# Seven block products for eight in five of 22 up-projection pairs, and shorter down chunks

## The chip, the cores and the metric

The kernel runs on one core of one Trainium2 chip. The metric is the device time of one execution in microseconds (us), the median of three runs. Five engines work side by side, each through its own queue in order: TensorE (PE, with PEld for its weight loads), VectorE (DVE), ScalarE (ACT), GpSimd (POOL) and SyncE (SP, which here only issues DMAs).

## The reference

Two layers of a decoder trunk on 512 tokens, width 1024, all in float32. Each layer is a mixer (state-space scan and stick-breaking attention in layer 0, a matrix-memory mixer in layer 1) and then a gated convolution FFN. The change touches only the FFN:

```python
def conv_ffn(h, up_w, conv_w, conv_b, down_w):
    u = causal_dwconv(h @ up_w, conv_w, conv_b)      # up_w: 1024 x 5632
    gate, val = jnp.split(u, 2, axis=-1)
    return (jax.nn.silu(gate) * val) @ down_w        # down_w: 2816 x 1024
...
        h = h + conv_ffn(rmsnorm(h, norm_w[layer, 1]), ffn_up_w[layer], ...)
```

## The kernel before

Activations lie as features on the 128 partitions and 512 tokens along the row. A float32 product is made of three fp32r matmuls (`mm3`): high part by high part, high by low, low by high. Every weight tile is therefore split first: ACT copies it into `hi`, DVE subtracts to get `lo`; `W_BUFS` = 5 such tiles can be ready ahead of PE, and two `raw` tiles receive them from DRAM.

**Up projection.** The 2816 gate and 2816 value columns are 22 tiles of 128 each; tile j of both makes one *pair*. A plain tile (`feat`) is 8 k-tiles times 3 matmuls of 512 columns, so a pair is 48 matmuls. DVE multiplies the result by the row factor `rb` (the norm), ACT and DVE make the width-3 convolution, ACT the SiLU, DVE the product of gate and value.

**Down projection.** For the first 16 of the 22 k-tiles, in two chunks of 8 (`CHUNKS`), the product is done in 2 x 2 blocks (two k-tiles, two output tiles, two halves of the tokens) with 7 block products for 8 (a Strassen form): `token_sums` makes the seven sums of the activations (`11`, `21`, `22`, `n1`, `n2`, `t3`, `t4`; tiles `B`, `s`, `F`, `G`), `weight_tiles` the sums of the weights (`P1` to `P4`; two of them begin as an accumulating DMA that POOL issues, two are DVE adds), and `down_blocks` runs, for each of four *slices* c (two output tiles), seven products of (k-tiles / 2) x 3 matmuls of 256 columns into PSUM tiles X, Y and Z. DVE adds each result to the residual `h` as it comes; as X and Y go on accumulating, such a read must be done before the next product into the same tile. The last 6 k-tiles (`REST`) are plain (`down_rest`).

The residual `h` (8 tiles) stays in SBUF throughout. All activations, sums and `P` tiles share 71 slots, which come free in the order in which they were asked for.

**What sets the order.** The program is recorded first, and `Recorder.order` then places every call: each engine takes, of the calls whose inputs are ready by the table of costs in the code, the one that was written first. The queues then run in that order; an SP row that waits holds every DMA behind it.

Of the kernel before, what the change touches and what calls it, by code (L numbers as in the profile page):

```python
# [15 lines left out]
F32 = mybir.dt.float32  # L16
F32R = mybir.dt.float32r
AF = mybir.ActivationFunctionType
ALU = mybir.AluOpType
# [3 lines left out]
P = 128  # L23
T = 512
NB = 4
KD = 8
EPS = 1e-6
FF = 22
# [4 lines left out]
def _feat(w):  # L33

    k, n = w.shape
    return list(w.reshape(k // P, P, n // P, P).transpose(2, 1, 0, 3))
# [48 lines left out]
def _ffn_units(i, l):  # L85
    u = []
    up = _feat(i["ffn_up_w"][l])
    dn = i["ffn_down_w"][l]
    for kind, n in FFN_PLAN:
        if kind == "up":  # L90
            u += [up[n], up[FF + n]]
        elif kind == "down":
            a, b = CHUNKS[n]

            t = dn[a * P : b * P].reshape((b - a) // 2, 2, P, 4, 2, P).transpose(3, 2, 4, 1, 0, 5)
            u += [x.reshape(P, 4, (b - a) // 2, P) for x in t]
        else:
            u += _feat(dn[REST * P :])
    return u

CHUNKS = [(0, 8), (8, 16)]
REST = 16
FFN_PLAN = [("up", j) for j in range(9)] + [("down", 0)] + [("up", j) for j in range(9, 17)] + [("down", 1)]
FFN_PLAN += [("up", j) for j in range(17, FF)] + [("rest", 0)]

X = lambda kind, *ns: [(kind, n) for n in ns]
# [161 lines left out]
class Recorder:  # L273
# [5 lines left out]
    def add(self, engine, method, args, kw):  # L279
        c = Call()  # L280
        c.engine, c.method, c.args, c.kw, c.i = engine, method, args, kw, len(self.calls)
        views = [a for a in args if isinstance(a, View)] + [a for a in kw.values() if isinstance(a, View)]
        c.outs, c.ins = views[:1], views[1:]
        c.func = next((a for a in args if a in TABLES), None) if method == "activation" else None
        c.cost = self.cost(c)
        self.calls.append(c)
# [162 lines left out]
class Net:  # L449
# [65 lines left out]
    def weight_tiles(self):  # L515

        v = self.nc.vector
        while self.wi < len(self.sizes):
            n, blocks = self.sizes[self.wi]
            if not blocks:  # L520
                yield self.split_weights([self.load_unit(self.raw_tile())])
                continue
            src, kb = self.next_unit(), n // 4
            r1, r2 = self.raw_tile(), self.raw_tile()[:, 0:kb]
            self.nc.sync.dma_start(r1, src[:, 0 : 2 * kb])
            p1, p2, p3, p4 = (self.slot(f"P{k}") for k in (1, 2, 3, 4))
            yield self.split_weights([r1])

            for p, i in ((p1, 3), (p3, 0)):
                self.nc.sync.dma_start(p, src[:, 2 * kb : 3 * kb])  # L530
                self.nc.gpsimd.dma_start(p, src[:, i * kb : (i + 1) * kb], accum_op=ALU.add)
            v.tensor_tensor(p2, p1, r1[:, 0:kb], op=ALU.add)
            yield self.split_weights([p2, p1])
            v.tensor_tensor(p4, p2, r1[:, kb : 2 * kb], op=ALU.add)
            self.nc.sync.dma_start(r2, src[:, 3 * kb : n])
            yield self.split_weights([p3, p4])
            yield self.split_weights([r2])
# [634 lines left out]


    def ffn(self, l, h, last):
        nc = self.nc
        xs, _, _, rb = self.norm(h, f"nw{l}1")
        pairs, ss, first = {}, [], None
        for kind, j in FFN_PLAN:
            if kind == "down":
                a, b = CHUNKS[j]  # L1180
                for c in range(4):
                    self.down_blocks([pairs[k] for k in range(a // 2, b // 2)], h, c)
                continue
            if kind == "rest":
                self.down_rest(ss, h, last)
                continue
            cc = []
            for part in range(2):
                n = j + part * FF
                ps = self.ps(("pj", "zz", "yy")[self.n % 3])  # L1190
                self.feat(ps, xs)
                u, c = self.slot("u"), self.slot("c")
                nc.vector.tensor_tensor(u, ps, rb, op=ALU.mult)
                nc.scalar.activation(c, u, AF.Identity, scale=self.param(f"fw{l}2", n), bias=self.param(f"fb{l}", n))
                for d in (1, 2):
                    nc.vector.scalar_tensor_tensor(c[:, d:T], u[:, 0 : T - d], self.param(f"fw{l}{2 - d}", n), c[:, d:T],
                                                   op0=ALU.mult, op1=ALU.add)
                cc.append(c)
            nc.scalar.activation(cc[0], cc[0], AF.Silu)
            nc.vector.tensor_tensor(cc[1], cc[0], cc[1], op=ALU.mult)  # L1200
            if j >= REST:
                ss.append(self.split(cc[1], "s"))
            elif j % 2:
                pairs[j // 2] = self.token_sums(first, cc[1])
            else:
                first = cc[1]

    def token_sums(self, c1, c2):

        v = self.nc.vector  # L1210
        a, b = slice(0, T // 2), slice(T // 2, T)
        t = self.slot("B11", F32R)
        self.nc.scalar.copy(t[:, a], c1[:, a])
        v.tensor_tensor(t[:, b], c1[:, a], t[:, a].bitcast(F32), op=ALU.subtract)
        s2 = self.split(c2, "s")
        f, g = self.slot("F"), self.slot("G")
        v.tensor_tensor(f[:, a], c1[:, a], c1[:, b], op=ALU.subtract)
        v.scalar_tensor_tensor(f[:, b], c2[:, b], -1.0, f[:, a], op0=ALU.mult, op1=ALU.subtract)
        fs = self.split(f, "F")
        v.tensor_tensor(g[:, a], c2[:, b], c1[:, b], op=ALU.subtract)  # L1220
        v.scalar_tensor_tensor(g[:, b], f[:, b], -1.0, c2[:, a], op0=ALU.mult, op1=ALU.subtract)
        gs = self.split(g, "G")
        half = lambda t, s: (t[0][:, s], t[1][:, s])
        return {"11": (t[:, a], t[:, b]), "21": half(s2, a), "22": half(s2, b),
                "n1": half(fs, a), "n2": half(fs, b), "t3": half(gs, a), "t4": half(gs, b)}

    def down_blocks(self, xs, h, c):

        v = self.nc.vector
        kb, n = len(xs) * P, T // 2
        a, b = slice(0, n), slice(n, T)
        X, Z, Y = (self.ps(t)[:, 0:n] for t in (("pj", "yy", "zz"), ("yy", "pj", "pj"))[c % 2])
        h1, h2 = h[2 * c], h[2 * c + 1]
        at = {"i": 0, "u": None}

        def product(ps, form, more=False):
            i = at["i"]  # L1240
            if i % 2 == 0:
                at["u"] = self.unit()
            hi, lo = at["u"]
            at["i"] = i + 1
            for k, x in enumerate(xs):
                s = slice(i % 2 * kb + k * P, i % 2 * kb + k * P + P)
                self.mm3(ps, (hi[:, s], lo[:, s]), x[form], not more and k == 0, k == len(xs) - 1, skip_group_check=more)

        add = lambda o, ps, op=ALU.add: v.tensor_tensor(o, o, ps, op=op)
        product(X, "11")  # L1250
        product(Z, "21")
        add(h1[:, a], X)
        product(X, "n2", True)
        add(h1[:, a], Z)
        product(Y, "n1")
        add(h1[:, b], X)
        product(X, "t3", True)
        add(h2[:, b], Y, ALU.subtract)
        product(Y, "22", True)
        add(h2[:, b], X, ALU.subtract)  # L1260
        product(X, "t4", True)
        add(h1[:, b], Y)
        add(h2[:, a], X, ALU.subtract)

    def down_rest(self, ss, h, last):
        nc = self.nc
        for c in range(8):
            ps = self.ps(("pj", "zz", "yy", "tt")[c % 4])
            self.feat(ps, ss)
            nc.vector.tensor_tensor(h[c], ps, h[c], op=ALU.add)  # L1270
            if last:
                nc.sync.dma_start(self.out[c], h[c])

    def load_x(self, a=0, b=KD):
        h = []
# [6 lines left out]
    def run(self):  # L1282
        nc = self.nc
# [4 lines left out]
        ps = self.ps()  # L1288
# [4 lines left out]
        h, raw = [], []  # L1293
# [4 lines left out]
        xs, w0 = [], []  # L1298
# [9 lines left out]
        xs, var, r, rb = self.norm(h, "nw00", xs)  # L1308
# [57 lines left out]
        h = S["h"]  # L1366
        yb = S.get("yb", [])
        yb += [self.split(self.ysb[k], "yb") for k in range(len(yb), 8)]
        for c in range(8):
            if ("b", c) in S:  # L1370
                pb, u = S["b", c]
# [3 lines left out]
                self.feat(pb, yb)  # L1375
            nc.vector.tensor_tensor(h[c], pb, h[c], op=ALU.add)
        S.clear()
        self.ffn(0, h, False)


        xs, var, r, rb = self.norm(h, "nw10")
# [23 lines left out]
        a, b, c = L1_CUTS  # L1405
# [13 lines left out]
        for c in range(8):  # L1419
            if c < OUT_SPLIT:  # L1420
                ps, u = begun[c]
                self.feat(ps, ys, u, tiles=range(4, 8))
            else:
                ps = self.ps(("pj", "zz", "yy", "tt")[c % 4])
# [59 lines left out]
```

## Time and profile before

| what | value |
|---|---|
| median of 3 runs | 1389.71 us (1389.37 to 1391.11) |
| profiled execution, own time | 1389.56 us |
| its span, first to last instruction | 1387.8 us |
| PE / DVE / ACT busy | 1376.7 / 1116.2 / 783.9 us |
| DMA | 147.96 MB, mean 107 GB/s |

A busy PE is a modelled figure, so the waits of PE are read from the chain and from the spacing of its groups. The FFN of layer 0 begins at about 463 us of the span and ends at about 811; that of layer 1 runs from about 1032 to the end.

### The profile page before, as it was taken

What the parts mean: (1) busy time and instruction counts of PE and PEld (TensorE: products, weight loads), DVE (VectorE), ACT (ScalarE), POOL (GpSimd) and SP (SyncE); (2) the same over time, 40 slices, a digit from 0 to 9 for tenths busy, and PEclk for the clock granted to TensorE, in tenths of its full rate; (3) what the DMA queues carried; (4) which work ended last, traced back from release to release, by engine and by line L of the source; (5) the groups of instructions that cost most, each with busy time, mean ns of one, the idle gap of its engine ahead of it and who ended that gap; (6) DMA issues with size and microseconds to landing.
All of it is one profiled execution on the core that took longest, in us unless ns stands there. A gap on an engine that the chain in (4) does not pass through costs nothing.

```text
span 1387.8 us, 20206 instructions
## 1 busy us (share of the span) xinstructions
PE 1376.7 (99%) x7491; PEld 1185.3 (85%) x7491; DVE 1116.2 (80%) x1963; ACT 783.9 (56%) x1325; POOL 87.1 (6%) x172
## 2 busy tenths in 40 slices
PE   9999999999999999999999999999999999999998
PEld 8898998989788888988898898888888899889887
DVE  7999889999997778878877657798758886888662
ACT  7798997786665444344434446776434444444440
POOL 0000001201120001000100000110000010010000
PEclk9999999999999999999999999999999999999999
DMA  6423223223312345243532225222234354443422
GB/s 220 130 77 112 86 78 98 70 83 132 98 46 91 101 127 137 92 138 113 129 122 95 81 82 171 77 92 89 65 106 126 102 129 129 122 133 95 137 68 84
DMA packets 53617, 147.96 MB, mean 107 GB/s; under 512 B 6136, under 2 KB 7160, under 8 KB 53520
## 3 DMA queue, kind: packets, MB, share of 16 engines
q1 hardware_dynamic: 48912, 138.29, 31.4%
q0 software_dynamic: 4608, 8.39, 3.7%
q8 instruction: 59, 0.97, 0.3%
q14 instruction: 38, 0.31, 0.1%
HBM read 141.36 MB, written 2.15 MB: 103 GB/s over the span
## 4 chain that ended last, share of the span: by engine, by line
PE 88%; DVE 5%; issue 3%; ACT 3%; POOL 1%; DMA 0%; SPq 0%; DVEq 0%; POOLq 0%; ACTq 0%
PE pj L436 43%; PE yy L436 26%; PE zz L436 14%; PE tt L436 5%; DVE gt L436 1%; DVE wt L436 1%; DVE lo L436 1%; DVE wTl L436 0%; ACT L436 0%; ACT Kh L436 0%; DMA h<-in_xT 0%; POOL wt L436 0%; ACT Q L436 0%; DVE ss L436 0%; ACT hi L436 0%
## 5 line engine op out<-in xcount | busy, mean ns | idle before, releaser
L436 ACT CAST hi<-raw 128x1024 fp32r<-128x1024 f32 (+2 forms) x236 | 227.8, 968 | 257.2 <-PE yy L436 58.6
L436 DVE TENSOR_TENSOR lo<-raw,hi 128x1024 fp32r<-128x1024 f32 (+2 forms) x236 | 263.8, 1120 | 25.2 <-ACT hi L436 24.5
L436 PE MATMUL pj<-xnh,hi 128*128 128x512 f32 x488 | 194.1, 398 | 0.0
L436 PE MATMUL pj<-xnh,lo 128*128 128x512 f32 x488 | 193.9, 397 | 0.0
L436 PE MATMUL pj<-xnl,hi 128*128 128x512 f32 x488 | 193.5, 396 | 0.0
L436 DVE SCALAR_TENSOR_TENSOR c<-u,pp,c 128x511 f32<-128x511 f32 (+2 forms) x212 | 158.0, 748 | 3.9 <-ACT c L436 1.6
L436 PE MATMUL yy<-xnl,hi 128*128 128x512 f32 x320 | 126.4, 395 | 0.0
L436 PE MATMUL yy<-xnh,lo 128*128 128x512 f32 x320 | 126.2, 394 | 0.0
L436 PE MATMUL yy<-xnh,hi 128*128 128x512 f32 x320 | 125.6, 392 | 0.0
L436 PE MATMUL pj<-lo,xnh 128*128 128x384 f32 (+2 forms) x320 | 108.6, 340 | 0.0
L436 PEld LDWEIGHTS pj<-xnh,lo 128*128 128x128 f32 x488 | 91.8, 188 | 19.1
L436 PEld LDWEIGHTS pj<-xnl,hi 128*128 128x128 f32 x488 | 91.8, 188 | 18.9
L436 PEld LDWEIGHTS pj<-xnh,hi 128*128 128x128 f32 x488 | 91.9, 188 | 18.8 <-issue 0.2
L436 PE MATMUL pj<-hi,xnl 128*128 128x384 f32 (+2 forms) x320 | 107.2, 336 | 0.0
L436 PE MATMUL pj<-hi,xnh 128*128 128x384 f32 (+2 forms) x320 | 106.8, 338 | 0.0
L436 ACT ACTIVATE c<-u,pp 128x512 f32<-128x512 f32 x100 | 81.1, 813 | 9.7 <-DVE u L436 8.3
L436 PE MATMUL zz<-xnl,hi 128*128 128x512 f32 x184 | 72.7, 395 | 0.0
L436 PE MATMUL zz<-xnh,lo 128*128 128x512 f32 x184 | 72.5, 394 | 0.0
L436 PE MATMUL zz<-xnh,hi 128*128 128x512 f32 x184 | 72.2, 392 | 0.0
L436 PEld LDWEIGHTS yy<-xnh,hi 128*128 128x128 f32 x320 | 60.2, 188 | 14.0
L436 PEld LDWEIGHTS yy<-xnl,hi 128*128 128x128 f32 x320 | 60.1, 188 | 13.9
L436 PEld LDWEIGHTS yy<-xnh,lo 128*128 128x128 f32 x320 | 60.1, 188 | 13.3
(418 smaller groups left out, 3330.7 us busy)
## 6 DMA issues: line engine op xcount, KB each, us to landing
raw<-in_w SPq DMA_DIRECT2D x168, 512.0 KB, 3.4
raw<-in_w SPq DMA_DIRECT2D x44, 384.0 KB, 3.1
P<-in_w SPq DMA_DIRECT2D x32, 256.0 KB, 5.6
P<-in_w POOLq DMA_DIRECT2D x32, 256.0 KB, 6.8
h<-in_xT SPq DMA_DIRECT2D x16, 256.0 KB, 4.7
E<-acsd SPq DMA_DIRECT2D x16, 256.0 KB, 3.9
raw<-in_w SPq DMA_DIRECT2D x16, 256.0 KB, 3.1
raw<-in_w SPq DMA_DIRECT2D x8, 264.0 KB, 2.7
```

The source lines that it names most:

```text
L436: getattr(getattr(nc, c.engine), c.method)(*(r(a) for a in c.args), **{k: r(v) for k, v in c.kw.items()})
```

## The change

In pairs 7, 10, 13, 16 and 19 (`UP_BLOCKS`) of each layer, gate and value tile together are the two outputs of a block product over k in four groups of two k-tiles: 7 products of 4 x 3 matmuls of 256 columns, 84 in all, stand for the 48 of 512 columns. For that, four `("x", n)` steps between the first up tiles scale `h` by the norm's weight and run `token_sums` on it (the parts `11`, `21`, `22` are views of the split `xn` that is there already; `F` and `G` are new). The weights of such a pair come through the block path of `weight_tiles`. Results are read out by ACT (four copies) and DVE (three adds), and then multiplied by `rb`.

The down projection becomes three chunks of 6 k-tiles and 4 plain ones. The residual goes to DRAM tiles `hd` when the FFN begins; each slice loads its two tiles, adds, and stores them back, and `down_rest` loads all eight.

```diff
+        if kind == "up" and n in UP_BLOCKS:
+            u.append(np.stack([up[m][:, k::2] for m in (n, FF + n) for k in range(2)], axis=1))
...
-CHUNKS = [(0, 8), (8, 16)]
-REST = 16
+CHUNKS = [(0, 6), (6, 12), (12, 18)]
+REST = 18
+UP_BLOCKS = (7, 10, 13, 16, 19)
...
+        hd = [self.dram.tile([P, T], F32, name=self.name("hd")) for _ in range(KD)]
+        for k in range(KD):
+            nc.sync.dma_start(hd[k], h[k])
...
+            if kind == "x":
+                hw = []
+                for k in (2 * j, 2 * j + 1):
+                    hw.append(self.slot("hw"))
+                    v.tensor_scalar(hw[-1], h[k], self.param(f"nw{l}1", k), None, op0=ALU.mult)
+                xb.append(self.token_sums(*hw, xs[2 * j], xs[2 * j + 1]))
...
                 for c in range(4):
-                    self.down_blocks([pairs[k] for k in range(a // 2, b // 2)], h, c)
+                    if c < 3:
+                        load(c + 1)
+                    self.down_blocks([pairs[k] for k in range(a // 2, b // 2)], *loaded[c], c)
+                    for e in range(2):
+                        nc.sync.dma_start(hd[2 * c + e], loaded[c][e])
...
+    def up_blocks(self, xs, rb, c):
+            if name in ("X1", "X2"):
+                nc.scalar.copy(u1[:, a if name == "X1" else b], ps)
+            elif name in ("Y1", "X4"):
+                nc.scalar.activation(u2[:, b if name == "Y1" else a], ps, AF.Copy, scale=-1.0)
+            elif name == "X3":
+                v.tensor_tensor(u2[:, b], u2[:, b], ps, op=ALU.subtract)
+            else:
+                o = u1[:, a if name == "Z" else b]
+                v.tensor_tensor(o, o, ps, op=ALU.add)
```

How the queues change, at three places. First PE, in the up projection. Before, a tile is 24 matmuls of 512 columns, of which these are the first five (`xnh`, `xnl` are the halves of the split activations; all have such names before the change):

```order
L436 MATMUL yy_6913<-xnh_5207,hi_6764 128x512
L436 MATMUL yy_6913<-xnl_5240,hi_6764 128x512
L436 MATMUL yy_6913<-xnh_5207,lo_6773 128x512
L436 MATMUL yy_6913<-xnh_5212,hi_6764 128x512
L436 MATMUL yy_6913<-xnl_5247,hi_6764 128x512
```

In pair 10 of the change, where the first block product (into `pj`) ends and the second (into `yy`) begins:

```order
L442 MATMUL pj_6881<-xnh_5382,hi_6740 128x256
L442 MATMUL pj_6881<-xnl_5398,hi_6740 128x256
L442 MATMUL pj_6881<-xnh_5382,lo_6751 128x256
L442 MATMUL yy_6901<-xnh_5216,hi_6740 128x256
L442 MATMUL yy_6901<-xnl_5251,hi_6740 128x256
L442 MATMUL yy_6901<-xnh_5216,lo_6751 128x256
```

The matmuls are half as wide, and 12 of them make a product where 24 made a tile. In the whole program PE gets 7911 matmuls for 7479.

Second DVE, in a down chunk of layer 0. Before (chunk 0, third slice; `h` rows read a product, `lo` rows split weights):

```order
L436 TENSOR_TENSOR lo_6500<-raw_6400,hi_6481 128x1024
L436 TENSOR_TENSOR h_4095<-h_4095,yy_6486 128x256
L436 TENSOR_TENSOR lo_6521<-P_1348_6449,hi_6505 128x512
L436 TENSOR_TENSOR h_4095<-h_4095,pj_6419 128x256
L436 TENSOR_TENSOR lo_6521<-P_1347_6154,hi_6505 128x512
L436 TENSOR_TENSOR lo_6550<-P_1349_6162,hi_6539 128x512
L436 TENSOR_TENSOR h_4107<-h_4107,zz_6524 128x256
L436 TENSOR_TENSOR h_4107<-h_4107,pj_6419 128x256
```

And after the change (chunk 1, third slice):

```order
L442 TENSOR_TENSOR P_1556_7492<-P_1555_7350,raw_7438 128x384
L442 TENSOR_TENSOR h_7196<-h_7196,yy_7409 128x256
L442 TENSOR_TENSOR P_1558_7507<-P_1556_7492,raw_7438 128x384
L442 TENSOR_TENSOR lo_7513<-raw_7438,hi_7490 128x768
L442 TENSOR_TENSOR lo_7526<-P_1556_7492,hi_7505 128x384
L442 TENSOR_TENSOR h_7196<-h_7196,pj_7406 128x256
L442 TENSOR_TENSOR h_7208<-h_7208,zz_7484 128x256
L442 TENSOR_TENSOR lo_7542<-P_1557_7366,hi_7518 128x384
L442 TENSOR_TENSOR h_7299<-h_7299,yy_7520 128x256
L442 TENSOR_TENSOR lo_7526<-P_1555_7350,hi_7505 128x384
L442 TENSOR_TENSOR B_1603_7533<-c_7269,B_1603_7533 128x256
```

The weight pieces are three quarters as wide, the reads of 256 columns are as wide as before, and there are more instructions in all: DVE gets 2249 for 1963.

Third SP, in chunk 0 of layer 0. Before, only weights stand in the queue there:

```order
L436 DMA raw_6210<-in_w 128x512
L436 DMA raw_6251<-in_w 128x1024
L436 DMA raw_6364<-in_w 128x512
L436 DMA raw_6400<-in_w 128x1024
L436 DMA raw_6488<-in_w 128x512
```

After, the stores of the residual stand between them:

```order
L442 DMA hd_5203<-h_5896 128x512
L442 DMA hd_5212<-h_5916 128x512
L442 DMA raw_6320<-in_w 128x768
L442 DMA P_1379_6337<-in_w 128x512
L442 DMA P_1381_6349<-in_w 128x512
L442 DMA hd_5253<-h_6000 128x512
L442 DMA raw_6385<-in_w 128x384
L442 DMA hd_5264<-h_6017 128x512
L442 DMA raw_6443<-in_w 128x1024
L442 DMA hd_5280<-h_6071 128x512
```

The first two `hd` rows are the stores of slice 0; the weights of slice 3 (`raw_6320`, `raw_6385`) and of pair 7 (`P_1379` on, `raw_6443`) are queued behind stores of slices 0 and 1. SP gets 532 DMAs for 352, of which 64 are stores to `hd` and 64 loads from it.

## Rows read from the trace of the kernel before

**Rows 1.** The page: busy engines, and the chain that ended last by engine.

```profile
PE 1376.7 (99%) x7491; PEld 1185.3 (85%) x7491; DVE 1116.2 (80%) x1963; ACT 783.9 (56%) x1325; POOL 87.1 (6%) x172
...
PE 88%; DVE 5%; issue 3%; ACT 3%; POOL 1%; DMA 0%; SPq 0%; DVEq 0%; POOLq 0%; ACTq 0%
```

**Rows 2.** Busy time of each engine in four stretches (windows).

```profile
core 0: us, PE busy (x) PEld busy (x) DVE busy (x) ACT busy (x) POOL busy (x), PEclk, DMA share, GB/s
463.00:785.70 322.70, 322.70 (x1723) 276.94 (x1723) 253.93 (x388) 143.19 (x198) 15.51 (x40) 1.00 0.39 113
10.00:20.00 10.00, 10.00 (x56) 9.80 (x56) 9.53 (x16) 10.00 (x23) 0.00 (x0) 1.00 0.71 274
30.00:40.00 10.00, 10.00 (x52) 8.29 (x50) 9.37 (x32) 5.62 (x11) 0.00 (x0) 1.00 0.40 137
610.00:640.00 30.00, 30.00 (x132) 24.34 (x130) 26.11 (x39) 15.48 (x22) 1.75 (x2) 1.00 0.43 123
```

**Rows 3.** Chain of waits, FFN of layer 0: start, length, what.

```profile
584.59 1.44 PE pj L436 x12
586.03 1.43 PE yy L436 x12
587.47 1.44 PE pj L436 x12
588.91 1.42 PE yy L436 x12
590.33 1.42 PE pj L436 x12
591.75 73.64 PE yy L436 x324
...
744.04 11.11 PE zz L436 x48
755.15 11.11 PE pj L436 x48
...
794.02 4.16 PE pj L436 x18
798.18 4.16 PE zz L436 x18
```

**Rows 4.** Timeline of DVE, FFN of layer 0: start, duration, instruction.

```profile
564.56 0.42 DVE L436 TENSOR_TENSOR h<-h,pj 128x256 f32<-128x256 f32 x1
564.90 0.41 DVE L436 TENSOR_TENSOR h<-h,yy 128x256 f32<-128x256 f32 x1
565.23 0.42 DVE L436 TENSOR_TENSOR F<-c 128x256 f32<-128x256 f32 x1
565.56 1.22 DVE L436 TENSOR_TENSOR lo<-raw,hi 128x1024 fp32r<-128x1024 f32 x1
566.70 0.69 DVE L436 TENSOR_TENSOR lo<-P,hi 128x512 fp32r<-128x512 f32 x1
567.30 0.41 DVE L436 TENSOR_TENSOR h<-h,pj 128x256 f32<-128x256 f32 x1
...
612.21 0.74 DVE L436 SCALAR_TENSOR_TENSOR c<-u,pp,c 128x511 f32<-128x511 f32 x1
612.87 0.68 DVE L436 TENSOR_TENSOR Fl<-F,Fh 128x512 fp32r<-128x512 f32 x1
...
773.05 0.95 DVE L436 TENSOR_TENSOR lo<-raw,hi 128x768 fp32r<-128x768 f32 x1
773.92 1.53 DVE L436 SCALAR_TENSOR_TENSOR c<-u,pp,c 128x511 f32<-128x511 f32 x2
```

**Rows 5.** DMA queues: bytes and share of 16 engines' span.

```profile
q1 hardware_dynamic: 48912, 138.29, 31.4%
q0 software_dynamic: 4608, 8.39, 3.7%
```

**Rows 6.** What SP's queue waited for: us in total, times, longest.

```profile
SPq L436 <- DVE lo L436: 868.8, 179, 25.3
SPq L436 <- DVE h L436: 98.0, 24, 9.2
```

**Rows 7.** DMA issues: KB each, median us to landing.

```profile
raw<-in_w SPq DMA_DIRECT2D x168, 512.0 KB, 3.4
h<-in_xT SPq DMA_DIRECT2D x16, 256.0 KB, 4.7
out_h<-h SPq DMA_DIRECT2D x8, 256.0 KB, 2.0
```

More of the change, by code (lines that the diff above doesn't have):

```diff
@@ L89, in _ffn_units @@
     for kind, n in FFN_PLAN:
-        if kind == "up":
+        if kind == "up" and n in UP_BLOCKS:
+            u.append(np.stack([up[m][:, k::2] for m in (n, FF + n) for k in range(2)], axis=1))
+        elif kind == "up":
             u += [up[n], up[FF + n]]
@@ L96, in _ffn_units @@
             u += [x.reshape(P, 4, (b - a) // 2, P) for x in t]
-        else:
+        elif kind == "rest":
             u += _feat(dn[REST * P :])
     return u
-CHUNKS = [(0, 8), (8, 16)]
-REST = 16
-FFN_PLAN = [("up", j) for j in range(9)] + [("down", 0)] + [("up", j) for j in range(9, 17)] + [("down", 1)]
-FFN_PLAN += [("up", j) for j in range(17, FF)] + [("rest", 0)]
+CHUNKS = [(0, 6), (6, 12), (12, 18)]
+REST = 18
+UP_BLOCKS = (7, 10, 13, 16, 19)
+FFN_PLAN = [("up", 0), ("up", 1), ("x", 0), ("up", 2), ("x", 1), ("up", 3), ("x", 2), ("up", 4), ("x", 3), ("up", 5)]
+FFN_PLAN += [("load", 0), ("up", 6), ("down", 0)] + [("up", j) for j in range(7, 12)]
+FFN_PLAN += [("load", 1), ("up", 12), ("down", 1)] + [("up", j) for j in range(13, 18)]
+FFN_PLAN += [("load", 2), ("up", 18), ("down", 2)] + [("up", j) for j in range(19, FF)] + [("rest", 0)]
 X = lambda kind, *ns: [(kind, n) for n in ns]
@@ L523, in weight_tiles @@
             src, kb = self.next_unit(), n // 4
-            r1, r2 = self.raw_tile(), self.raw_tile()[:, 0:kb]
+            r1, r2 = self.raw_tile()[:, 0 : 2 * kb], self.raw_tile()[:, 0:kb]
             self.nc.sync.dma_start(r1, src[:, 0 : 2 * kb])
-            p1, p2, p3, p4 = (self.slot(f"P{k}") for k in (1, 2, 3, 4))
+            p1, p2, p3, p4 = (self.slot(f"P{k}", n=kb) for k in (1, 2, 3, 4))
             yield self.split_weights([r1])
@@ L1174, in ffn, with load @@
     def ffn(self, l, h, last):
-        nc = self.nc
+        nc, v = self.nc, self.nc.vector
         xs, _, _, rb = self.norm(h, f"nw{l}1")
-        pairs, ss, first = {}, [], None
-        for kind, j in FFN_PLAN:
+        hd = [self.dram.tile([P, T], F32, name=self.name("hd")) for _ in range(KD)]
+        for k in range(KD):
+            nc.sync.dma_start(hd[k], h[k])
+        pairs, ss, first, xb, loaded = {}, [], None, [], {}
+        def load(c):
+            loaded[c] = self.slot("h"), self.slot("h")
+            for e in range(2):
+                nc.sync.dma_start(loaded[c][e], hd[2 * c + e])
+        for kind, j in FFN_PLAN:
+            if kind == "x":
[4 more added lines that the diff above has]
+                xb.append(self.token_sums(*hw, xs[2 * j], xs[2 * j + 1]))
+                continue
+            if kind == "load":
+                load(0)
+                continue
             if kind == "down":
@@ L1181, in ffn @@
                 for c in range(4):
-                    self.down_blocks([pairs[k] for k in range(a // 2, b // 2)], h, c)
+                    if c < 3:
+                        load(c + 1)
+                    self.down_blocks([pairs[k] for k in range(a // 2, b // 2)], *loaded[c], c)
+                    for e in range(2):
+                        nc.sync.dma_start(hd[2 * c + e], loaded[c][e])
                 continue
             if kind == "rest":
-                self.down_rest(ss, h, last)
-                continue
-            cc = []
+                return self.down_rest(ss, hd, last)
+            us, cc = [None, None], []
+            if j in UP_BLOCKS:
+                us = self.up_blocks(xb, rb, j)
             for part in range(2):
[L1189 to L1193, printed above, removed]
+                n, u, c = j + part * FF, us[part], self.slot("c")
+                if u is None:
+                    ps = self.ps(("pj", "zz", "yy")[self.n % 3])
+                    self.feat(ps, xs)
+                    u = self.slot("u")
+                    v.tensor_tensor(u, ps, rb, op=ALU.mult)
                 nc.scalar.activation(c, u, AF.Identity, scale=self.param(f"fw{l}2", n), bias=self.param(f"fb{l}", n))
                 for d in (1, 2):
-                    nc.vector.scalar_tensor_tensor(c[:, d:T], u[:, 0 : T - d], self.param(f"fw{l}{2 - d}", n), c[:, d:T],
-                                                   op0=ALU.mult, op1=ALU.add)
+                    v.scalar_tensor_tensor(c[:, d:T], u[:, 0 : T - d], self.param(f"fw{l}{2 - d}", n), c[:, d:T],
+                                           op0=ALU.mult, op1=ALU.add)
                 cc.append(c)
             nc.scalar.activation(cc[0], cc[0], AF.Silu)
-            nc.vector.tensor_tensor(cc[1], cc[0], cc[1], op=ALU.mult)
+            v.tensor_tensor(cc[1], cc[0], cc[1], op=ALU.mult)
             if j >= REST:
@@ L1206, in ffn, with token_sums @@
                 first = cc[1]
-    def token_sums(self, c1, c2):
+    def token_sums(self, c1, c2, s1=None, s2=None):
         v = self.nc.vector
         a, b = slice(0, T // 2), slice(T // 2, T)
[L1212 to L1215, printed above, removed]
+        half = lambda t, s: (t[0][:, s], t[1][:, s])
+        if s1 is None:
+            t = self.slot("B11", F32R)
+            self.nc.scalar.copy(t[:, a], c1[:, a])
+            v.tensor_tensor(t[:, b], c1[:, a], t[:, a].bitcast(F32), op=ALU.subtract)
+            s11, s2 = (t[:, a], t[:, b]), self.split(c2, "s")
+        else:
+            s11 = half(s1, a)
         f, g = self.slot("F"), self.slot("G")
@@ L1222, in token_sums, with blocks @@
         gs = self.split(g, "G")
-        half = lambda t, s: (t[0][:, s], t[1][:, s])
-        return {"11": (t[:, a], t[:, b]), "21": half(s2, a), "22": half(s2, b),
+        return {"11": s11, "21": half(s2, a), "22": half(s2, b),
                 "n1": half(fs, a), "n2": half(fs, b), "t3": half(gs, a), "t4": half(gs, b)}
-    def down_blocks(self, xs, h, c):
-        v = self.nc.vector
+    def blocks(self, xs, c, read):
         kb, n = len(xs) * P, T // 2
-        a, b = slice(0, n), slice(n, T)
         X, Z, Y = (self.ps(t)[:, 0:n] for t in (("pj", "yy", "zz"), ("yy", "pj", "pj"))[c % 2])
[L1236 to L1240, printed above, removed]
+        steps = (X, "11", "X1"), (Z, "21", "Z"), (X, "n2", "X2"), (Y, "n1", "Y1"), (X, "t3", "X3"), (Y, "22", "Y2"), (X, "t4", "X4")
+        for i, (ps, form, name) in enumerate(steps):
             if i % 2 == 0:
-                at["u"] = self.unit()
-            hi, lo = at["u"]
-            at["i"] = i + 1
+                hi, lo = self.unit()
+            more = name[1:] > "1"
             for k, x in enumerate(xs):
@@ L1247, in product, with down_blocks, read, down_rest @@
                 self.mm3(ps, (hi[:, s], lo[:, s]), x[form], not more and k == 0, k == len(xs) - 1, skip_group_check=more)
[L1249 to L1267, printed above, removed]
+            read(name, ps)
+    def down_blocks(self, xs, h1, h2, c):
+        a, b = slice(0, T // 2), slice(T // 2, T)
+        to = {"X1": h1[:, a], "Z": h1[:, a], "X2": h1[:, b], "Y2": h1[:, b], "Y1": h2[:, b], "X3": h2[:, b], "X4": h2[:, a]}
+        def read(name, ps):
+            op = ALU.add if name in ("X1", "Z", "X2", "Y2") else ALU.subtract
+            self.nc.vector.tensor_tensor(to[name], to[name], ps, op=op)
+        self.blocks(xs, c, read)
+    def up_blocks(self, xs, rb, c):
+        nc, v = self.nc, self.nc.vector
+        a, b = slice(0, T // 2), slice(T // 2, T)
+        u1, u2 = self.slot("u"), self.slot("u")
+        def read(name, ps):
+            if name in ("X1", "X2"):
[4 more added lines that the diff above has]
+                v.tensor_tensor(u2[:, b], u2[:, b], ps, op=ALU.subtract)
+            else:
+                o = u1[:, a if name == "Z" else b]
+                v.tensor_tensor(o, o, ps, op=ALU.add)
+        self.blocks(xs, c, read)
+        for u in (u1, u2):
+            v.tensor_tensor(u, u, rb, op=ALU.mult)
+        return u1, u2
+    def down_rest(self, ss, hd, last):
+        nc, h = self.nc, [self.slot("h") for _ in range(KD)]
+        for c in range(KD):
+            nc.sync.dma_start(h[c], hd[c])
+        for c in range(KD):
             ps = self.ps(("pj", "zz", "yy", "tt")[c % 4])
@@ L1272, in down_rest @@
                 nc.sync.dma_start(self.out[c], h[c])
+        return h
     def load_x(self, a=0, b=KD):
@@ L1377, in run @@
         S.clear()
-        self.ffn(0, h, False)
+        h = self.ffn(0, h, False)
         xs, var, r, rb = self.norm(h, "nw10")
```

## The prediction

> **What bounds the kernel now.** I read the page first: PE is shown busy for 99% of the span, and 88% of the chain that ended last is PE, 5% DVE [rows 1]. The change lies in the two FFNs alone, so next come the windows: over the FFN of layer 0 up to its plain rest (463.0 to 785.7 us) PE is busy for all 322.7 us, DVE for 253.9 (79%), ACT for 143.2 (44%), and the DMA share is 0.39 [rows 2]. As a busy PE is modelled, I checked it in the chain: there the FFN is nothing but PE groups, end to end, each at one pace: a plain tile pair of 48 matmuls takes 11.11 us, 18 plain matmuls of the rest 4.16, and five block products of 12 half-wide matmuls in a row take 591.75 - 584.59 = 7.16, so 1.432 each [rows 3]. The FFN is bound by PE's matmuls, with no gap to see. So matmul time that goes is time gained, as long as DVE, which has 21% left, takes the work that comes.
>
> **What PE loses.** A block pair is 7 products of 12 matmuls: 7 x 1.432 = 10.02 us for 11.11, 1.09 less; five of them 5.4 per FFN. Down before: 2 chunks x 4 slices x 7 products = 56 x 1.432 = 80.2, and 8 x 4.16 = 33.3 plain: 113.5. After: 84 products of 9 matmuls, 84 x 1.074 = 90.2, and 8 x 12/18 x 4.16 = 22.2: 112.4, 1.1 less. Together 6.5 per FFN, **13.1 us** for both. With the single products of 1.42 and 1.44 instead of 1.432 it is 14.0 or 12.4 [rows 3].
>
> [...]
>
> **What DVE gains.** The price of an instruction in a full queue is the distance from its start to the next start: 0.34 us for 256 columns, 0.60 for 512, 1.14 for 1024, 0.87 for 768, 0.66 for one of the convolution's steps [rows 4]. For 384 columns I take 0.47, on the line between 0.34 and 0.60.
> - A block pair against a plain one: splitting weights 3 x 1.14 + 0.60 for 2 x 1.14, two weight sums 1.20, three reads 1.02; the multiplications by `rb` stay two of 512. 3.96 more, ten times: 39.6.
> - Eight `x` steps: two scalings, four half sums (1.36), two splits (1.20). A scaling of 512 columns has no row of its own here: between 0.34 and 0.66; I take 0.35. 3.3 each: 26.1 (31 at the upper end).
> - Down: a slice had 3 x 1.14 + 0.60 + 2 x 0.60 + 7 x 0.34 = 7.6; now 3 x 0.87 + 0.47 + 2 x 0.47 + 7 x 0.34 = 6.4. Eight slices were 60.8, twelve are 76.8: 16.0 per FFN, 32.0.
> - One more pair of k-tiles through `token_sums` 4.6; narrower weights of the rest -4.3.
>
> Sum 98, **49 us per FFN**. In the stretch measured above DVE comes to about 305 us, PE to 322.7 - 5.4 + 10.0 (the third chunk, which the rest gives back later) = 327.3: **93% for 79%**. PE stays the longer one, by 7%.
>
> **Where that is tight.** Not evenly. While PE runs a chunk's 28 shorter products (30.1 us), DVE has 28 reads (9.5), the weights of three slices (12.1; the first slice's are ready ahead), the weights of the block pair that follows each of the three chunks (5.2) and the end of the pair before (two convolution steps, a product, two half sums: 2.6): 29.4, or 98%. The block pairs further on are easier: one with its two plain neighbours is about 29.4 us of DVE beside 10.0 + 22.2 of PE. The `x` steps stand beside seven plain pairs, 72 beside 78. So the six chunks are where PE will wait. How full can DVE be before PE feels it? In the trace it reaches 95.3% beside a PE that shows no idle time (10 to 20 us), 93.7% in another stretch, 87% in the plain up projection [rows 2]. At 95.3% the 29.4 take 30.85, 0.75 over PE's 30.1, six times 4.5 us; at 93.7% they take 31.4, 7.7 us in all; at full load nothing. I take 95.3%, the highest that a row shows: **4.5 us** lost, with 0 and 7.7 as ends.
>
> **What costs nothing, and what covers it.** ACT's new copies, and its share of the splits, fall on an engine that is 44% busy there. The reads of X and Y are pressed into 1.07 us products for 1.43: a read waits for DVE's instruction ahead (up to 1.14) and takes 0.42 [rows 4], which would not fit, but the order puts products of the next slice between, as it did before; without that each of the 84 reads between products of one tile could cost some 0.3 us. The `hd` traffic is 128 transfers of 256 KB, 33.6 MB, and the weights grow by 9.4 MB. At the rate of the hardware queue (31.4% of 1387.8 us for 138.29 MB, 3.15 us per MB) and of the accumulating one (6.1 us per MB) [rows 5] the share in the FFN rises from 0.39 to about 0.65. The trace has 0.71 at 274 GB/s beside a PE without gaps [rows 2]. A store in SP's queue waits for DVE's last add of its slice, and weights wait behind it; DVE's adds have held that queue 24 times already, up to 9.2 us [rows 6]. The cover is the order: slice 3's weights stand behind the stores of slices 0 and 1, so are free to go two slices (15 us) before their use, against 3.4 us to land and 1.14 for DVE's part of the split [rows 4, 7]. The loads of `hd` stand a chunk ahead; a load like them took 4.7, a store 2.0 [rows 7].
>
> **Sum.** 1389.56 (the profiled execution's own time; 1.76 more than its span and 0.15 below the median) - 13.1 + 4.5 = **1381.0 us**, 0.6% faster.
>
> **The rivals.**
> 1. *DVE keeps up everywhere.* For it: its work fits in every stretch I summed. Against: 98% in the chunks with no spare. 1389.56 - 13.1 = **1376.5**.
> 2. *DVE becomes the bound, and the kernel is slower.* Place: the FFNs as a whole. If a queue in order, which also waits for PE and ACT, is never fuller than some share, 305 us of work takes 305/share. The change has lost its 6.5 us per FFN when that exceeds 333.8, at 91.4%. At 90% it is 338.9, 11.6 over per FFN: **1399.7**. For it: the plain up projection runs at 87%. Against: there DVE is waiting for PE, not full; and 95.3% has been reached. [...]
> 3. *The stores hold the weights.* Place: SP's queue in the six chunks. It decides where weights come later than the 10.7 us (five tiles of two products each) that are ready ahead; if a chunk then stood for 3 us, 18 us, **1394.5**. Against it the 15 us above.
>
> **How the numbers follow.** Chances: the forecast 0.52 (1378 to 1385, the ends of the loss and of the product's pace), rival 1 0.28, rival 2 0.12 (of which a third within the bound of no change or just under it), rival 3 0.08. Rival 1 reaches down to 1375.6 (product at 1.42); the range 1375.5 to 1387.5 takes in the forecast, rival 1 and the mild part of rival 2 and leaves out under 0.2. About 0.2% (2.8 us) is what a measurement of this kernel can tell from no change. Faster by more: 0.52 + 0.28 and a little of the others, 0.82; within: 0.07; slower: 0.11.
>
> **What would show it.** Right: matmuls of 256 columns in the up projection 119 ns apart; 84 in about 10.0 us; DVE at 90 to 95% from 463 us to the rest; the chain in the FFN still PE, with short pieces of DVE `lo` or `h` in the down chunks only. Wrong: gaps of PE in the up stretches, waits of PE's weight loads for `lo` of over 5 us per FFN, waits of ACT `hi` for DMA `raw` behind `hd` stores, or a first plain matmul of the rest that waits for `h`. The prediction fails if DVE's new instructions cost their durations, or if the share of DMA slows the weights.

## The result, and the profile after

The kernel before took 1389.62 us (median of 4 runs, 1389.37 to 1391.11), the changed one **1402.72 us** (4 runs, 1400.18 to 1405.94): a ratio of 1.0093, 95% interval 1.0071 to 1.0116. The forecast was 1381.0, so the change is slower where faster was expected. The profiled execution of after took 1400.18 us with a span of 1398.5.

The page of after, busy engines and the chain that ended last (by engine, then by line; compare [rows 1]):

```profile
PE 1374.7 (98%) x7923; PEld 1202.2 (86%) x7923; DVE 1202.5 (86%) x2249; ACT 832.3 (60%) x1473; POOL 120.6 (9%) x208
...
PE 81%; DVE 8%; DMA 3%; issue 3%; ACT 3%; POOL 1%; SPq 0%; DVEq 0%; ACTq 0%; POOLq 0%
PE pj L442 46%; PE yy L442 19%; PE zz L442 11%; PE tt L442 5%; DMA raw<-in_w 3%; DVE lo L442 2%; DVE h L442 1%; DVE gt L442 1%; DVE P L442 1%; DVE wt L442 1%; ACT hi L442 1%; DVE wTl L442 0%; ACT L442 0%; DMA h<-in_xT 0%; ACT Kh L442 0%
```

PE's share of the chain fell from 88% to 81%, and a line stands in it that before had 0%: DMA `raw<-in_w`, the load of a weight tile, 3% (some 40 us). (In such lines DMA `a<-b` is a transfer, `SPq` the queue of SP, and `issue` time in which an engine waited for nothing that the profile shows.) DVE is at 86%, not at its end. The windows of after are over the FFN of layer 0 to its rest, over the second down chunk, and over a stretch in it in which PE stands, with the one behind it (columns as in [rows 2]):

```profile
463.00:793.00 330.00, 323.56 (x1951) 287.90 (x1950) 287.03 (x508) 163.83 (x264) 32.18 (x59) 0.99 0.60 169
627.00:673.00 46.00, 43.73 (x344) 42.53 (x343) 36.03 (x74) 18.59 (x33) 6.93 (x8) 0.96 0.83 218
647.00:652.00 5.00, 2.81 (x15) 2.39 (x14) 3.83 (x8) 2.79 (x6) 1.07 (x2) 0.82 0.93 243
652.00:657.00 5.00, 5.00 (x39) 5.00 (x38) 4.23 (x10) 1.56 (x2) 0.00 (x0) 0.84 0.51 166
```

Before, PE filled its stretch of this FFN to 322.70 of 322.70 us [rows 2]; now 6.4 of 330 are empty, and a DMA share of 0.60 over the FFN is 0.83 in the chunk and 0.93 around the stand. Over both FFNs the idle times in PE's rows add up to 11.1 us, each ended by ACT `hi`, DVE `lo` or DVE `h`. The stand itself, first in the chain of waits, then ACT's row for the same tile:

```profile
641.17 0.56 DVE P L442
641.74 0.02 SPq L442
641.76 0.04 issue
641.80 6.21 DMA raw<-in_w
...
648.98 0.47 DVE P L442
649.45 0.88 DVE lo L442
650.33 0.04 issue
650.37 1.86 PE yy L442 x7
```

```profile
648.09 0.83 ACT L442 CAST hi<-raw 128x768 fp32r<-128x768 f32 x1 [4.56 <-DMA raw<-in_w]
```

This is slice 3 of the chunk. The load of its first weight tile is issued at 641.80, directly behind a weight sum of the slice ahead (DVE `P`, 641.17 to 641.73), because that sum is the last reader of the `raw` tile which the load writes. It lands 6.2 us later; ACT, which has stood for 4.56 us, casts it, DVE makes `lo`, and PE goes on at 650.37. Load, cast, sums, split and release make a loop, and only two `raw` tiles go round in it. The next load of SP follows at 650.35, right behind the split of the landed tile (DVE `lo`, to 650.33), so the loop took 8.55 us, for a slice that lasts 7 x 1.074 = 7.5 us on PE. The same chain, a DVE `P`, then some 6 us of DMA `raw`, stands at 552.43, 740.75 and 750.35. PE's rows show what the stand cost beyond itself (timeline):

```profile
648.97 0.51 PE L442 MATMUL yy<-B,hi 128*128 128x256 f32 x2 [1.54 <-ACT hi L442]
...
650.37 0.58 PE L442 MATMUL yy<-B,lo 128*128 128x256 f32 x1 [0.65 <-DVE lo L442]
...
652.25 0.42 PE L442 MATMUL pj<-Gh,hi 128*128 128x256 f32 x1
652.46 0.41 PE L442 MATMUL pj<-Gl,hi 128*128 128x256 f32 x1
```

Behind the two gaps matmuls of 256 columns start 0.21 us apart for 0.12: the granted clock is 0.82 from 647 to 652 us, 1.00 up to 649.0 and 0.50 from 650.2 on. Fourteen matmuls take 3.15 us for 1.67. Three stretches of the FFNs, each behind such gaps, stand at a granted clock of 0.50 (from 650.2 to 653.5, 749.2 to 752.5 and 1230.5 to 1233.8 us); at these paces some 5 of their 9.9 us are lost, an estimate. Over the whole span the granted clock is 0.996 (before 1.0).

The DMA issues between 627 and 673 us (KB each, median us to landing; before, the 512 KB load took 3.4, over the whole span [rows 7] and between 627 and 673 us alike):

```profile
hd<-h SPq DMA_DIRECT2D x8, 256.0 KB, 4.9
raw<-in_w SPq DMA_DIRECT2D x4, 512.0 KB, 5.7
...
P<-in_w POOLq DMA_DIRECT2D x4, 192.0 KB, 6.8
raw<-in_w SPq DMA_DIRECT2D x2, 384.0 KB, 4.6
...
h<-hd SPq DMA_DIRECT2D x2, 256.0 KB, 7.1
```

### The profile page after: what moved, and what is told of

It reads as the page before. It is cut to its first block, busy times and chain, and to the rows that moved or that the text cites. A ratio compares the mean times of both kernels' runs of the same rounds, so it can differ in the third digit from the quotient of the medians.

```text
span 1398.5 us, 21954 instructions
## 1 busy us (share of the span) xinstructions
PE 1374.7 (98%) x7923; PEld 1202.2 (86%) x7923; DVE 1202.5 (86%) x2249; ACT 832.3 (60%) x1473; POOL 120.6 (9%) x208
## 4 chain that ended last, share of the span: by engine, by line
PE 81%; DVE 8%; DMA 3%; issue 3%; ACT 3%; POOL 1%; SPq 0%; DVEq 0%; ACTq 0%; POOLq 0%
PE pj L442 46%; PE yy L442 19%; PE zz L442 11%; PE tt L442 5%; DMA raw<-in_w 3%; DVE lo L442 2%; DVE h L442 1%; DVE gt L442 1%; DVE P L442 1%; DVE wt L442 1%; ACT hi L442 1%; DVE wTl L442 0%; ACT L442 0%; DMA h<-in_xT 0%; ACT Kh L442 0%
## 5 line engine op out<-in xcount | busy, mean ns | idle before, releaser
L442 ACT CAST hi<-raw 128x1024 fp32r<-128x1024 f32 (+3 forms) x252 | 225.5, 897 | 274.0 <-PE pj L442 95.6
L442 DVE TENSOR_TENSOR lo<-raw,hi 128x1024 fp32r<-128x1024 f32 (+3 forms) x252 | 259.1, 1029 | 25.8 <-ACT hi L442 24.8
L442 PE MATMUL pj<-xnh,hi 128*128 128x512 f32 (+1 forms) x592 | 228.6, 386 | 0.0
L442 PE MATMUL pj<-xnh,lo 128*128 128x512 f32 (+1 forms) x592 | 227.6, 385 | 0.0
L442 PE MATMUL pj<-xnl,hi 128*128 128x512 f32 (+1 forms) x592 | 227.4, 384 | 0.0
L442 ACT CAST hi<-P 128x384 fp32r<-128x384 f32 (+1 forms) x136 | 70.0, 541 | 48.4 <-PE yy L442 12.4
L442 DVE TENSOR_TENSOR lo<-P,hi 128x384 fp32r<-128x384 f32 (+1 forms) x136 | 78.0, 591 | 4.4 <-ACT hi L442 4.4
L442 PE MATMUL yy<-xnh,hi 128*128 128x512 f32 (+1 forms) x200 | 74.6, 373 | 2.6 <-ACT hi L442 2.6
L442 PE MATMUL yy<-xnh,lo 128*128 128x512 f32 (+1 forms) x200 | 74.8, 374 | 1.4 <-DVE lo L442 1.4
L442 PE MATMUL yy<-xnl,hi 128*128 128x512 f32 (+1 forms) x200 | 74.3, 371 | 0.0
```

Source lines behind the costliest of these rows:

```text
L442: getattr(getattr(nc, c.engine), c.method)(*(r(a) for a in c.args), **{k: r(v) for k, v in c.kw.items()})
```

## The experiments

Three theories: A, the residual's transfers lengthen the loads or hold them on SP; B, DVE is full in the chunks and frees things late; C, two `raw` tiles are too few for the shorter slices. Each edit is made to the changed kernel where nothing else is said. The medians of before in the four groups of runs were 1389.49, 1389.60, 1389.63 and 1389.46.

No edit changes one thing alone. `Recorder.order` places all calls anew, from its costs and the number of copies of each tile, so every version has its own order in the queues. With three `raw` tiles the order of SP differs from 34 us of the span on, long before the first FFN. What an edit gives back in all is therefore not the price of one cause; the waits in the traces are the better witness.

### No residual traffic in the chunks

```diff
-                    if c < 3:
-                        load(c + 1)
-                    self.down_blocks([pairs[k] for k in range(a // 2, b // 2)], *loaded[c], c)
-                    for e in range(2):
-                        nc.sync.dma_start(hd[2 * c + e], loaded[c][e])
+                    self.down_blocks([pairs[k] for k in range(a // 2, b // 2)], *loaded[0], c)
```

> The changed kernel without the residual's loads and stores inside the down chunks: each chunk loads the tiles of slice 0 and adds all four slices to them, nothing is stored back (the output is wrong; PE, ACT and DVE have the same instructions). Theory A (transfers: the residual's loads and stores fill the DMA engines and SP's queue, so weights land in some 6 us for 3.4): 1377 to 1383 us, PE in the down chunks without gaps, raw tiles landing in 3 to 4 us there. Theory B (DVE is full in the chunks and frees the raw tiles late): 1397 to 1403, gaps where they were. Theory C (two raw tiles are too few; the load begins when DVE's last weight sum is done): 1392 to 1400, since the load still begins late but lands sooner.

Measured 1384.32 us, ratio 0.9965 (0.9952 to 0.9978): 18.4 us less than the change, a little above what theory A expected and well below B and C. In the same 46 us of the trace the 512 KB load lands in 4.3 us:

```profile
raw<-in_w SPq DMA_DIRECT2D x6, 512.0 KB, 4.3
```

Without the residual's traffic most of the loss is gone. Whether by its bytes or its place in SP's queue this doesn't tell.

### DVE reads 8 of 256 columns

Only in the down chunks: DVE's seven reads of a slice take 8 columns each.

```diff
-            self.nc.vector.tensor_tensor(to[name], to[name], ps, op=op)
+            self.nc.vector.tensor_tensor(to[name][:, 0:8], to[name][:, 0:8], ps[:, 0:8], op=op)
```

> The changed kernel with DVE reading only 8 of 256 columns of each down product (the residual misses the rest, the output is wrong): 84 reads of 0.34 us become some 0.08, 22 us of DVE per FFN less, 7 per chunk, DMA as in the change. Theory A: 1396 to 1403. Theory B: 1377 to 1383, chunks without gaps. Theory C: 1380 to 1392, as the weight sums come sooner but the load still waits for them.

Measured 1407.38 us, 1.0134 (1.0107 to 1.0161), above the ranges of all three theories: nothing came back. Its window over the same chunk, and the DVE row at the same stand:

```profile
627.00:673.00 46.00, 42.23 (x340) 40.76 (x339) 30.36 (x76) 18.77 (x34) 6.97 (x8) 1.00 0.85 218
```

```profile
647.49 0.56 DVE L442 TENSOR_TENSOR P<-P,raw 128x384 f32<-128x384 f32 x1 [2.70 <-DMA P<-in_w]
```

DVE is busy for 30.4 us here against 36.0 (a read of 8 columns in a full queue has the next start 0.07 or 0.08 us behind its own: 650.10, 650.18, 650.25), and PE is no better off (42.2 against 43.7): DVE waits for a transfer. B falls.

### The down part alone

```diff
-UP_BLOCKS = (7, 10, 13, 16, 19)
-FFN_PLAN = [("up", 0), ("up", 1), ("x", 0), ("up", 2), ("x", 1), ("up", 3), ("x", 2), ("up", 4), ("x", 3), ("up", 5)]
+UP_BLOCKS = ()
+FFN_PLAN = [("up", j) for j in range(6)]
```

> Only the down part of the change: three chunks of 6, the residual in DRAM, all 22 pairs plain, no x steps (output as the reference). PE alone would be 2.2 us under the kernel before. If the weights of the block pairs behind the chunks (7 pieces of 256 KB each, DVE 5.2 us) are what overloads the chunks: 1386 to 1389. If the residual's traffic alone does it (theory A): 1396 to 1402.

Measured 1390.01 us, 1.0004 (0.9994 to 1.0014): the same as before, and between the two ranges expected. PE has no gap, with all of the residual's traffic (window):

```profile
463.00:785.70 322.70, 322.70 (x1765) 278.66 (x1765) 264.97 (x447) 146.65 (x220) 20.73 (x46) 1.00 0.53 159
```

So the traffic and the shorter slices together lose no time where all pairs are plain. The `x` steps are gone here too, so this run doesn't part them from the block pairs.

### Three raw tiles

```diff
-RAW_BUFS = 2
+RAW_BUFS = 3
```

> The changed kernel with three raw tiles for two, 4 KB more per partition, otherwise the same (output as the reference). Theory C: 1378 to 1386, the load of a slice's first weights no longer waits for the last weight sum of the slice before. Theories A and B: 1396 to 1403.

Measured 1381.77 us, 0.9946 (0.9931 to 0.9961): 20.9 us less than the change, as theory C expected, and faster than both kernels. The loads still land late (the 512 KB ones in 5.6 us in the same stretch); they start earlier. The chunk of the stand above begins at 627.9 here, for 627.4. SP's load of slice 3's first weights, ACT's cast of it and the product that stood for it:

```profile
636.57 0.33 SPq L442 DMA_DIRECT2D raw<-in_w  x1
```

```profile
644.80 0.84 ACT L442 CAST hi<-raw 128x768 fp32r<-128x768 f32 x1 [1.04 <-PE yy L442]
```

```profile
647.08 0.40 PE L442 MATMUL yy<-B,hi 128*128 128x256 f32 x2
```

The load goes out 5.2 us earlier than at 641.80, ACT no longer waits for it, and PE starts the product without a gap (which load belongs to slice 3 follows from the order of the loads; the trace leaves buffer numbers out). Of the 17.5 us between the two profiled executions 13.3 lie in the FFNs, 3.1 ahead of the first. What is left is read from a gap of PE in the first chunk, which ends behind DVE `h`. PE's row, then DVE's timeline and the chain there:

```profile
557.07 0.39 PE L442 MATMUL pj<-Gh,hi 128*128 128x256 f32 x1 [1.58 <-DVE h L442]
```

```profile
555.53 0.69 DVE L442 TENSOR_TENSOR P<-P,raw 128x512 f32<-128x512 f32 x1 [2.66 <-DMA P<-in_w]
556.13 0.55 DVE L442 TENSOR_TENSOR lo<-P,hi 128x384 fp32r<-128x384 f32 x1
556.60 0.41 DVE L442 TENSOR_TENSOR h<-h,pj 128x256 f32<-128x256 f32 x1
```

```profile
543.36 4.75 DMA P<-in_w
...
548.66 6.84 DMA P<-in_w
555.50 0.02 issue
555.53 0.04 DVE P L442
```

The read that PE needs is only queued behind a weight sum, which waits for tile P1: a load of 4.75 us, and behind it the accumulating load of 6.84, 12.1 us from the first issue. DVE is empty while PE waits for it.

### Three raw tiles and no residual traffic

The two edits above together.

> The change with three raw weight tiles, and with the loads and stores of the residual in the 12 down chunks left out (each chunk accumulates into the first slice's two tiles, so the output is not the reference's). Each alone gave 1381.8 (three raw tiles) and 1384.3 us (no residual traffic) against 1402.7. If both remove the same wait (the loop load, split, weight sums, release of a slice's first raw tile against its 7.5 us), the second adds next to nothing: 1379 to 1382. If they remove two different losses, of 18.4 and 20.9 us, the sum would be far below what TensorE's instructions take (about 1374): it cannot show in full, and the time would be at 1374 to 1377.

Measured 1376.32 us, 0.9904 (0.9889 to 0.9918), below the range for one wait and in the one for two losses. Each still adds to the other, 5.5 and 8.0 us; alone they give 20.9 and 18.4, so most of the 26.4 us goes with either edit. The page's chain, and the windows over the FFN and a chunk:

```profile
PE 87%; DVE 8%; ACT 2%; issue 2%; DMA 0%; POOL 0%; SPq 0%; DVEq 0%; ACTq 0%; POOLq 0%
```

```profile
463.00:785.70 322.70, 322.54 (x1967) 287.27 (x1966) 290.75 (x511) 164.72 (x266) 31.19 (x58) 1.00 0.52 139
530.00:560.00 30.00, 30.00 (x257) 30.00 (x256) 28.55 (x61) 13.93 (x27) 2.59 (x3) 1.00 0.52 144
```

With DVE busy for 28.55 of 30 us (95.2%), PE has no gap.

### The kernel before with three raw tiles

> The kernel before, with a third raw weight tile and nothing else. Its slices last 10.0 us, longer than the loop that frees a raw tile, so by the loop theory it has nothing to gain: 1389 to 1390, the same within 0.1%. If a third raw tile is worth something by itself (weights of the attention parts, say), it would show here at 1385 or below, and the gain of the change with three raw tiles would not be proof of the loop.

Measured 1390.14 us, 1.0002 (0.9993 to 1.0012): in total a third tile is worth nothing here. The profiled execution shows a sum behind this zero: the first FFN begins 2.2 us earlier than before, and the two FFNs are 2.0 and 1.3 us longer (from the norm's `var` to the last add; one execution of each).

### Short stores

```diff
-                        nc.sync.dma_start(hd[2 * c + e], loaded[c][e])
+                        nc.sync.dma_start(hd[2 * c + e][:, 0:8], loaded[c][e][:, 0:8])
```

> The change with two raw tiles as it is, but each of the chunks' residual stores writes 8 of its 512 columns (the output is not the reference's). The loads, the order on SP's queue and every semaphore stay; only half of the residual's bytes in the chunks go. If it is the bytes that stretch a weight load from 3.4 to some 6 us, a good part comes back: 1388 to 1396. If it is the place of a weight load behind stores that wait for the accumulation in SP's order, the time stays at 1399 to 1404.

Measured 1393.59 us, 1.0028 (1.0018 to 1.0038): half of the residual's bytes in the chunks gone, and 9.1 of the 18.4 us come back. The 512 KB load lands in 4.0 us. SP's order did not stay, as expected, though: where after issues a `raw` load (543.43) and then two of `P`, this version issues a load of `P` first (541.97, `raw` at 542.85). So bytes are what fits, and order is not ruled out.

### Stores from ScalarE

```diff
-                        nc.sync.dma_start(hd[2 * c + e], loaded[c][e])
+                        nc.scalar.dma_start(hd[2 * c + e], loaded[c][e])
```

> The change with two raw tiles, but the chunks' residual stores are issued by ScalarE instead of SP, all bytes as they are. If a weight load is late because it stands behind stores on SP that wait for VectorE's accumulation, the loads go earlier and a good part of the 20.9 us comes back: 1385 to 1395. If it is the bytes and the two raw tiles, nothing comes back, and ScalarE's casts may be held behind the stores: 1400 to 1406.

Measured 1403.05 us, 1.0093 (1.0063 to 1.0124): nothing came back, as expected if the place in SP's queue is not the cause. With the stores off SP's queue the chain's DMA share passes from `raw` to `P`:

```profile
PE pj L442 46%; PE yy L442 19%; PE zz L442 11%; PE tt L442 5%; DMA P<-in_w 4%; DVE gt L442 1%; DVE lo L442 1%; DVE wt L442 1%; ACT hi L442 1%; ACT E L442 1%; DVE wTl L442 0%; DMA raw<-in_w 0%; DMA E<-mrow 0%; DVE P L442 0%; ACT L442 0%
```

With three raw tiles as well:

> Three raw tiles and the chunks' stores on ScalarE. With three raw tiles 5.5 us are left between the full traffic (1381.8) and none (1376.3). If SP's order makes the sums' loads (tiles P1 and P3) late, 1377 to 1380. If it is the bytes, 1381 to 1384, or more if ScalarE's casts wait behind the stores.

Measured 1386.73 us (10 runs, 1379.71 to 1392.65), 0.9975 (0.9953 to 0.9997): 5 us worse than three raw tiles alone, above both ranges, and the runs lie 13 us apart, against 1.4 us there. What spreads them was not settled.

### Block pairs elsewhere, and more of them

```diff
-UP_BLOCKS = (7, 10, 13, 16, 19)
+UP_BLOCKS = (8, 11, 14, 17, 20)
```

> The change with two raw tiles, the five block pairs at 8, 11, 14, 17 and 20 for 7, 10, 13, 16 and 19, so that a plain pair stands between a down chunk and the first block pair behind it, and block pairs 11 and 17 stand a plain pair ahead of the next chunk. If the loop of the raw tiles inside the down chunks is what fails, the place of the pairs hardly matters: 1399 to 1405. If the loss needs the chunk's residual traffic and the block pair's weights at the same time, much of it goes: 1388 to 1395.

Measured 1406.78 us, 1.0121 (1.01 to 1.0143): above both ranges, and not better. With three raw tiles and `UP_BLOCKS = (8, 10, 14, 16, 20)`:

> Three raw tiles, and the block pairs at 8, 10, 14, 16 and 20 for 7, 10, 13, 16 and 19, so that a plain pair (two 512 KB weight tiles, no sums, no accumulating load) stands behind each down chunk and no block pair directly ahead of one. With three raw tiles and the pairs as in the change 1381.8 were measured, of which 5.5 us go without residual traffic. If those 5.5 us come from a block pair's sums loading at the same time as the last slices of a chunk, they shrink: 1377.5 to 1380.5. If they come from the slices inside a chunk alone, the place of the pairs changes nothing: 1381 to 1383. With a block pair only one plain pair behind another (8 and 10, 14 and 16), as in the version with seven pairs (1407.3), it may also lose: 1384 to 1392.

Measured 1391.11 us, 1.0013 (1.0004 to 1.0023): all of the gain is lost, at the upper end of the last case. With three raw tiles and `UP_BLOCKS = (7, 9, 11, 13, 15, 17, 19)`:

> Three raw weight tiles, and seven block pairs per FFN (7, 9, 11, 13, 15, 17, 19) for five. TensorE saves 1.09 us more per pair, 4.4 us over the two FFNs. If three raw tiles have ended the weights' lateness for block pairs outside the chunks, 1377.5 to 1379.5. If the transfers are at their end (every block pair brings two more accumulating loads into a stretch that is already full), the gain is eaten: 1381 to 1386.

Measured 1407.32 us, 1.0130 (1.0112 to 1.0148): 25.5 us worse than with five pairs, though PE has 4.4 us less to do (an estimate, four pairs of 1.09); far outside both expectations. Lengths in the chain of waits of the version with seven pairs:

```profile
542.84 4.24 DMA P<-in_w
547.63 7.58 DMA P<-in_w
564.00 6.49 DMA raw<-in_w
```

The chain with five pairs has the two loads of P1 in a row as well (above), and the one with moved pairs has loads of `P` and of `raw` too. In both versions with moved or added pairs and three raw tiles, block pairs stand with one plain pair between them instead of two. That this spacing is the cause was not tried by itself.

## Why the prediction was wrong

**The step that failed** is "What costs nothing, and what covers it": a DMA share "from 0.39 to about 0.65" over the FFN, and weights "free to go two slices (15 us) before their use, against 3.4 us to land". The share over the FFN came out near (0.60), but the traffic stands in the chunks. By the prediction's own prices (3.15 and 6.1 us per MB [rows 5]) a slice of after has 0.983 MB of weights on SP's queue (384 KB, 2 x 192, 192), 0.393 MB accumulating and 1.049 MB of residual: 3.1 + 2.4 + 3.3 = 8.8 us of the DMA engines in a slice of 7.5 us, 117%. A slice of before had 1.311 and 0.524 MB, 7.3 us in 10.0: 73%. The same sum without the stores is 7.15 us, 95%, and without any residual 5.5, 73%. The times with two raw tiles follow it in equal steps: 1402.7, 1393.6, 1384.3. The sum is an estimate, worked out after the fact from prices that are means over the span; the measured share in the chunk is 0.83, not full. The equal steps are measured.

**What the cover left out** is the `raw` tile. Ahead of the `hi` and `lo` tiles stand only two of them, and a block unit's first one is held until DVE's last weight sum has read it. The order would let the loads go two slices ahead; the tiles don't: the loop closed in 8.55 us with a landing of 6.2. ACT `hi` waiting for DMA `raw` is the sign of being wrong that the prediction itself had named. A third tile gave back 20.9 us, nothing in total in the kernel before, and 8.0 where the traffic is gone.

The profiled FFNs of after are 9.0 and 9.2 us longer than those of the version without both waits (354.6 and 355.4 for 345.6 and 346.2); PE's idle times, 11.1, and the lower clock, some 5, make up most of that. Another 4.8 us lie ahead of the first FFN, which begins at 462.23 for 457.43; the third tile changes the order of the queues there, and what these 4.8 us come from was not traced.

**Why it needs the block pairs.** The down part alone has the same slices and traffic, and lost nothing. What follows is argued, not shown: a chunk's excess, some 5 us by the sum above, fits into the 10.7 us of tiles ready ahead if plain pairs then fill them up again. A block pair behind the chunk brings 1.84 MB (512, 4 x 256 and 256 KB) in 10.0 us, a plain pair 1.05 MB (2 x 512 KB) in 11.1. The gap at 647 to 650 us is in the last slice's weights, where that reserve would be gone.

**TensorE's term, -13.1 us,** held in the main: with both waits gone the kernel takes 1376.32, 13.3 below before, and rival 1 had 1376.5. That the two agree to 0.2 is in part luck. In that trace the FFNs are 5.8 and 5.5 us shorter (from the norm's `var` to the last add) for the 6.5 summed, 11.3 in all, and 2.5 fell ahead of the first one, for which the prediction had nothing. The pace that the sum had from the rows came out, 117 to 119 ns for a matmul of 256 columns (products of nine in the chain of after):

```profile
654.08 1.05 PE zz L442 x9
655.96 1.07 PE pj L442 x9
```

The interval of the measured saving, 11.4 to 15.4 us, holds the 13.1.

**DVE's term, +4.5 us,** is wrong: at 95.2% in a chunk DVE delayed nothing there, and in both FFNs of that trace PE waits for it for 0.3 us (over the 322.7 us from 463 us on PE is idle for 0.16 in all). That the version with three raw tiles ended at 1381.77, 0.8 from the forecast, is chance: its 5.5 us over the floor go with the residual's transfers, not with DVE. DVE's work was put too high as well: 290.75 us in the 322.7 from 463 us on, so some 295 in the 327.3 for which 305 were summed. Rival 2 falls with it: the version at 1376.32 has all of the 286 added instructions of DVE. Nor did DVE's new instructions cost their durations: in the chunk of after two reads of 256 columns, at 640.04 and 640.37 us, last 0.41 and 0.42 us, and each has the next start 0.33 us behind its own.

**Rival 3, the stores that hold the weights,** was nearest in its sign and place (six chunks, weights late), but not in its mechanism: stores on another queue changed nothing, stores almost without bytes did (with another order as well). Its condition, weights later than the reserve, was right; its price was set without the landing time under load and without the clock: some 5 of the 26.4 us over the floor go with the granted clock of 0.50, by the estimate above.

**The down part's 1.1 us per FFN** did not show: the down part alone is at 1.0004. Its interval leaves out a gain of 2.2 us (0.9984), although PE has no gap in the window above. In the profiled execution the FFN of layer 0 is 1.2 us shorter than before, that of layer 1 0.8 longer, and the stretch between them 1.1 longer; why stays open.

## What to carry to other kernels

A transfer that is added to one stage is priced against that stage, not against a mean over a loop: bytes per slice times the queue's own us per MB, over the slice's length (here the measured share was 0.60 over the FFN and 0.83 in the chunk). When a step gets shorter, the loop of each buffer behind it (load, read, last reader, release) must get shorter too (here 8.55 us for a slice of 7.5); look for the tile with the fewest copies and follow it to its last reader. If a load grows slower under load (here 5.7 us for 3.4), one more copy of that tile can be worth more than the change itself: here 1381.77 us for 1402.72. And where a program orders its queues by a model, an edit that should change one thing moves others too: compare the orders before a difference is put down to it.

## What the runs showed that was not expected

- The landing of a 512 KB load went from 3.4 us [rows 7] to 5.7 beside the residual's traffic, at 218 GB/s and a DMA share of 0.83, well short of 1; without that traffic it was 4.3.
- The granted clock fell behind short gaps: after idle times of PE of 1.54 and 0.65 us it was 0.50 from 650.2 to 653.5 us, and matmuls ran 0.21 us apart for 0.12.
- The engine that a gap is put down to need not be late by its own work: a gap of PE ended by DVE `h` came out of 2.66 us in which DVE itself, two instructions earlier, waited for a load.
